# One hybrid mLSTM and windowed-attention layer: the load of the spread row factors queued behind the store of an attention block

## The chip, the cores and the metric

The kernel runs on one core of one Trainium2 chip, in one launch. The metric is device time in microseconds (us); lower is better. Several executions were timed, and one more was recorded by the hardware profiler.

## What is computed

The reference is one layer of a bidirectional encoder on a sequence of 4096 tokens of width 1024, in float32:

```python
hn = rms_norm(x, norm_w)
proj = hn @ w_in                     # 3856 columns
# group A: 4 heads x 128, short conv + SiLU on q and k, gated matrix memory
#          (chunks of 128), one scan in each direction, summed
# group B: 8 query heads / 2 key-value heads x 64, keys with |i - j| <= 128,
#          T5 bias, a sink logit per head
y = concatenate([y_a, y_b])          # each gated by silu of its own columns
out = rms_norm(x + y @ w_out, final_norm_w)
```

The change lies in the first pass, which makes group B's attention.

## The kernel before, in words

Float32 products are made of three (or two) float32r products of high and low parts, so TensorE has most of the work. There are three passes. `pass1` normalizes x, splits it into a high and a low part, makes q, k, v and the gate columns of group B, runs the attention, and writes two things to DRAM: the split, transposed x (`xT_d`) for the later passes, and the attention results (`at_d`), one [128, 512] block for each of 32 query blocks. Later passes make group A and the output.

**The steady loop of pass 1** (lines 608 to 620) runs over b = 0 to 12. x is handled in blocks of 256 tokens (16 of them), queries in blocks of 128 (two per x block), and attention in slots: one slot is one query block and one key-value head. In iteration b:

- `spread(b + 3)` (line 245) loads the 256 row factors of x block b+3 (the reciprocal root mean squares) from the DRAM buffer `rs_d` into all 128 partitions of the tile `rsb`. In iteration 0 it stands ahead of the loop (line 607).
- `load_rows(b + 4)` (line 222) loads rows of x (`xr`), and `norm_rows(b + 4)` (line 232) takes their squares on ScalarE, the factor on DVE and GpSimd, and writes it to `rs_d` with two small DMAs from GpSimd (line 243). Transposing the factors over partitions is what this trip through DRAM is for.
- A1: slots 4b and 4b+1, between the matmuls of `qproj(b + 1)` (line 523). `scale_raw(b + 3)` (line 251), on GpSimd, multiplies the raw, already transposed x (`xraw`) by `rsb`.
- A2: slots 4b+2 and 4b+3, between `kproj(b + 2)` and `vproj(b + 2)`. `splits(b + 3)` (line 257) splits the scaled `xraw` into `xT` (ScalarE line 263, GpSimd line 264), stores it to `xT_d` from GpSimd (line 277), and after its second and its fourth part loads a half of the next block's raw x (`load_raw(b + 4, h)`, line 229, SyncE, 512 KB each).

**The attention of a slot** is scores (line 358), softmax (361 to 375), transposes (386), and the product with v into one PSUM bank, `op` (line 400; the tag has one buffer). A slot's product is made in the slot behind it. ScalarE copies one half of `op` into the tile `ab` (line 412), and DVE adds the other half (line 413), which empties the bank. `ab` has one buffer. After the second head of a query block SyncE stores `ab` to `at_d` (line 415). The copy for the next query block must wait until that store has landed.

**The rings.** `x4` has 14 buffers, which `xT`, `xraw` and the transposed probabilities `pt` share; `rsb` has two buffers.

**What sets the order.** TensorE runs in the order of the code. On the other engines, SyncE's queue of loads and stores among them, a planner chooses the order; each engine then runs its list in order, and an instruction that waits holds all behind it on its queue. `behind(c, ins)` ties the instructions traced in its block to come after `ins` in their engine's list; it adds no wait on the hardware, and with `None` it does nothing. So SyncE's list between two stores is what the planner made of `spread`, `load_raw`, `load_rows` and the stores.

Of the kernel before, what the change touches and what calls it, by code (L numbers as in the profile page):

```python
# [122 lines left out]
def behind(c, ins):  # L123
    return c.tc.issue_after(ins.ins) if ins is not None else ExitStack()
# [43 lines left out]
def pass1(c):  # L168
    nc, tc, A = c.nc, c.tc, c.A
    NB = 16  # L170
    with ExitStack() as es:
# [42 lines left out]
        RAW, RSB, LAST = {}, {}, {}  # L214
# [30 lines left out]
        def spread(b):  # L245
            if b >= NB:
                return
            RSB[b] = wk.tile([128, 256], F32, tag="rsb", bufs=2, name=f"rsb{b}")
            nc.sync.dma_start(RSB[b], c.rs_d[b].partition_broadcast(128))

        def scale_raw(b):
            with behind(c, LAST["pool"]):
# [138 lines left out]
        def att_o(sl, i):  # L391
            n, kv = sl // 2, sl % 2
            js = ST[sl][1]
            if i >= len(js):
                return
            if i == 0:
                OP[sl] = c.ps("c", [128, 512], f"op{sl}")
            op, pt, vt = OP[sl], PT.pop((sl, i)), V[n - 1 + js[i]][:, kv, :]
            for z in range(2):
                nc.tensor.matmul(op, vt, pt[:, z, :], start=(i == 0 and z == 0),  # L400
                                 stop=(i == len(js) - 1 and z == 1))
            if i < len(js) - 1:
                return
            if kv == 0:
                AB[n] = wk.tile([128, 4, 128], F32, tag="ab", bufs=1, name=f"ab{n}")
            ab = AB[n]
            a = slice(0, 64) if kv == 0 else slice(64, 128)
            o = slice(64, 128) if kv == 0 else slice(0, 64)
            ov = op.rearrange("p (h g q) -> p h g q", h=2, g=4)
            av = ab.rearrange("p g (h q) -> p h g q", h=2)  # L410
            with tc.high_priority(offset=EV):
                nc.scalar.copy(av[a], ov[o])
                nc.vector.tensor_add(av[a], ov[a], av[a])  # L413
            if kv:
                nc.sync.dma_start(c.at_d[n], ab.rearrange("p g q -> p (g q)"))

        def slot(sl):
            T = lambda i: (lambda: att_t(sl, i))
            O = lambda i: (lambda: att_o(sl - 1, i))
            Sc = lambda g: (lambda: att_a(sl + 2, g))  # L420
            p = [Sc(0), O(0), Sc(1), T(0), O(1), Sc(2), T(1), O(2), Sc(3), T(2)]
            if sl == 0:
                p = [Sc(0), Sc(1), T(0), Sc(2), T(1), Sc(3), T(2)]
            if sl + 2 >= 2 * NCH:
                p = [O(0), T(0), O(1), T(1), O(2), T(2)]
            return p
# [175 lines left out]
        with behind(c, LAST["gather"]):  # L602
            load_rows(3)
            for h in range(2):
                load_raw(3, h)
        norm_rows(3, LAST["cast"])
        spread(3)
        for b in range(NB - 3):
            if b:
                spread(b + 3)  # L610
            load_rows(b + 4)
            s1 = slot(4 * b + 1)
            A1 = slot(4 * b) + [lambda: norm_rows(b + 4, LAST["act"])]
            A1 += s1[:5] + [lambda: scale_raw(b + 3)] + s1[5:]
            A2 = slot(4 * b + 2) + slot(4 * b + 3)
            interleave(qproj(b + 1), A1)
            f2, tu = kproj(b + 2) + vproj(b + 2), splits(b + 3)
            for p, u in zip((12, 20, 28, 36)[::-1], tu[::-1]):
                f2.insert(p, u)
            interleave(f2, A2)  # L620
        c.x7 = XT
        pieces = []
        for sl in range(4 * (NB - 3), 4 * NB):
            pieces += slot(sl)
        pieces += [(lambda i=i: att_o(2 * NCH - 1, i)) for i in range(3)]
        hooks = [(40, lambda: w2_load(0, 0)), (80, lambda: gate1(c, wk)), (100, lambda: gate2(c, wk)),
                 (104, lambda: w2_load(1, 512)), (113, lambda: gate3(c, wk)), (113, lambda: w2_load(2, 1024))]
# [898 lines left out]
```

## Time and profile before

| | us |
|---|---|
| median of 3 runs (2235.1 to 2237.13) | 2236.47 |
| the profiled execution's own time | 2239.41 |
| its span | 2237.7 |
| TensorE busy | 2168.3 (97%) |
| DVE, ScalarE, GpSimd busy | 1408.1, 1075.6, 609.5 |

The span is that of one profiled execution, from its first instruction to its last. An engine is busy while it computes; waiting and issuing DMAs is not counted. The granted clock is the share of full speed at which TensorE may run. SyncE (SP, or SPq for its queue) only issues DMAs here. A DMA has three moments: its issue, the time when its data moves, and its landing, of which a semaphore tells.

### The profile page before, as it was taken

To read this page: it belongs to the slowest core of one execution; us is meant where nothing else is said; L and a number is where in the kernel's file an instruction comes from. 1 tells how busy PE (TensorE), PEld (TensorE's weight loads), DVE (VectorE), ACT (ScalarE), POOL (GpSimd) and SP (SyncE) were. 2 spreads that over 40 slices of the span, in tenths; PEclk is the share of its full clock that TensorE was granted. 3 is DMA by queue.
4 is the path that set the end of the run, shared out by engine and by line. 5 is a ranking of instruction groups with operands and counts; after the bars stand their busy time and mean duration, and the time that the engine had idled before them with its cause. 6 is when DMAs were issued, how large, how long until landed. Compare 5 with 4: busy or idle time off the path is not lost.

```text
span 2237.7 us, 35209 instructions
## 1 busy us (share of the span) xinstructions
PE 2168.3 (97%) x12226; PEld 1879.7 (84%) x12226; DVE 1408.1 (63%) x3090; ACT 1075.6 (48%) x2711; POOL 609.5 (27%) x1059
## 2 busy tenths in 40 slices
PE   7999999999999999999999999999999999999997
PEld 6899999998788888888887888888888888888886
DVE  5677777777864665566567555555554443867776
ACT  5787787777743343334345343434443321333323
POOL 2555555553212211221122111111111111112222
PEclk9999999999999999999999999999999999999999
DMA  7542434422314442444166967876785899667774
GB/s 246 170 169 93 170 105 163 146 89 81 100 60 146 156 131 68 158 155 136 64 216 180 315 211 233 246 232 209 237 245 187 283 357 297 184 182 191 191 190 139
DMA packets 249126, 398.98 MB, mean 178 GB/s; under 512 B 21971, under 2 KB 128467, under 8 KB 248948
## 3 DMA queue, kind: packets, MB, share of 16 engines
q1 hardware_dynamic: 220628, 303.57, 43.5%
q0 software_dynamic: 28176, 92.96, 12.8%
q8 instruction: 96, 1.57, 0.3%
q14 instruction: 82, 0.67, 0.1%
q10 hardware_dynamic: 144, 0.20, 0.0%
HBM read 275.99 MB, written 120.67 MB: 177 GB/s over the span
## 4 chain that ended last, share of the span: by engine, by line
PE 71%; DMA 12%; DVE 5%; issue 5%; ACT 3%; POOL 2%; SPq 0%; POOLq 0%; DVEq 0%; ACTq 0%
PE up L855 15%; PE zp L1147 7%; PE op L1147 7%; PE qp L523 7%; PE v2p L828 7%; DMA xr<-x 5%; DMA at_d<-ab 3%; PE op L400 3%; PE zbp L158 3%; PE zbp L160 3%; PE zbp L159 3%; PE num L1100 2%; PE num L1099 2%; PE tp L386 2%; PE sp L358 2%
## 5 line engine op out<-in xcount | busy, mean ns | idle before, releaser
L855 PE MATMUL up<-xb,w 128*128 128x512 f32 x1344 | 338.5, 396 | 0.0
L1313 PE MATMUL o<-wo,yo 128*128 128x512 f32 (+1 forms) x1356 | 312.3, 392 | 0.0
L1313 PEld LDWEIGHTS o<-wo,yo 128*128 128x128 f32 x1356 | 253.2, 188 | 59.2
L855 PEld LDWEIGHTS up<-xb,w 128*128 128x128 f32 x1344 | 243.7, 188 | 47.2
L873 DVE SCALAR_TENSOR_TENSOR qk<-U,cw,qk 128x512 f32<-128x512 f32 x256 | 190.1, 754 | 92.5 <-ACT qk L871 88.6
L523 PE MATMUL qp<-xT,wqb 128*128 128x256 f32 x1536 | 246.5, 291 | 0.0
L523 PEld LDWEIGHTS qp<-xT,wqb 128*128 128x128 f32 x1536 | 218.3, 193 | 9.0 <-issue 0.9
L1147 PE MATMUL op<-w,xs 128*128 128x512 f32 x720 | 202.7, 409 | 2.9 <-ACT hs L1114 2.9
L1147 PE MATMUL zp<-w,xs 128*128 128x512 f32 x720 | 188.2, 402 | 2.3 <-DVE z L1156 2.3
L828 PE MATMUL v2p<-w,xb 128*128 128x512 f32 x672 | 158.1, 395 | 1.8 <-DMA xb<-xT_d 1.8
L1147 PEld LDWEIGHTS zp<-w,xs 128*128 128x128 f32 x720 | 131.0, 189 | 29.3 <-DVE z L1156 2.8
L828 PEld LDWEIGHTS v2p<-w,xb 128*128 128x128 f32 x672 | 125.9, 188 | 32.7 <-DMA xb<-xT_d 3.4
L1114 ACT ACTIVATE hs<-num,r 128x128 f32<-128x128 f32 x128 | 46.9, 367 | 213.8 <-DVE r L1111 185.2
L361 DVE CUSTOM_DVE_ANT_0 s<-sp,G 128x320 f32<-128x320 f32 (+1 forms) x256 | 122.7, 480 | 42.5 <-PE sp L358 39.3
L400 PE MATMUL op<-pt,v 128*128 128x512 f32 x376 | 122.2, 406 | 26.3 <-DVE ab L413 26.3
L1147 PEld LDWEIGHTS op<-w,xs 128*128 128x128 f32 x720 | 126.9, 190 | 24.3 <-ACT E L1068 3.3
L389 DVE TENSOR_TENSOR pt<-tp,pt 128x512 fp32r<-128x512 f32 x188 | 129.2, 688 | 26.1 <-ACT pt L388 24.7
L370 ACT ACTIVATE s<-s,st 128x320 f32<-128x320 f32 (+1 forms) x256 | 139.7, 549 | 10.1 <-DVE st L368 9.4
L388 ACT CAST pt<-tp 128x512 fp32r<-128x512 f32 x188 | 109.8, 586 | 59.0 <-PE tp L386 57.0
L358 PE MATMUL sp<-kk,q 128*128 128x320 f32 (+2 forms) x512 | 118.9, 314 | 0.0
L386 PE MATMUL tp<-ident,s 128*128 128x128 f32 x752 | 113.8, 274 | 1.5 <-DVE pt L389 1.2
L158 PE MATMUL zbp<-xc,w 128*128 128x512 f32 x256 | 101.5, 397 | 0.0
(273 smaller groups left out, 4444.0 us busy)
## 6 DMA issues: line engine op xcount, KB each, us to landing
xc<-xT_d SPq DMA_DIRECT2D x64, 512.0 KB, 7.9
xs<-xT_d SPq DMA_DIRECT2D x120, 256.0 KB, 6.3
xT_d<-xT POOLq DMA_DIRECT2D x104, 256.0 KB, 6.4
xb<-xT_d SPq DMA_DIRECT2D x48, 514.0 KB, 10.0
E<-m_d SPq DMA_DIRECT2D x64, 256.0 KB, 4.8
W<-w_d SPq DMA_DIRECT2D x64, 256.0 KB, 5.7
y<-y_d SPq DMA_DIRECT2D x32, 512.0 KB, 3.4
out<-xr POOLq DMA_DIRECT2D x31, 512.0 KB, 3.9
```

What stands on the lines that cost most here:

```text
L158: nc.tensor.matmul(out, wl, xh, start=first, stop=False)
L358: nc.tensor.matmul(sp[:, lo:hi], qt, kk[:, kv, z, col - 128 + lo:col - 128 + hi], start=(z == 0), stop=(z == 1))
L370: nc.scalar.activation(ps[g][:, kept(g)], ps[g][:, kept(g)], AF.Exp, bias=ng[:, g:g + 1], accum_out=rs[:, g:g + 1])
L386: nc.tensor.transpose(tp[:, g * 128:(g + 1) * 128], ps[g][:, j * 128:(j + 1) * 128], c.ident)
L389: nc.vector.tensor_sub(pt[:, 1, :], tp, f32(pt[:, 0, :]))
L400: nc.tensor.matmul(op, vt, pt[:, z, :], start=(i == 0 and z == 0), stop=(i == len(js) - 1 and z == 1))
L523: nc.tensor.matmul(qp, wq[k // 2][:, k % 2, w, m * 128:m * 128 + 128], x[k], start=(k == 0 and j == 0), stop=(k == KT - 1 and j == 2))
L828: nc.tensor.matmul(vp, a, wv[k // 2][:, k % 2, m, :], start=(k == 0 and j == 0), stop=(k == KT - 1 and j == 2))
L855: nc.tensor.matmul(up[:, 0:hi - lo], w[k // 2][:, k % 2, a, cs], x, start=(k == 0 and j == 0), stop=(k == KT - 1 and j == 2))
L873: nc.vector.scalar_tensor_tensor(acc, U[:, t:t + 512], cw[:, cm, t:t + 1], acc, ALU.mult, ALU.add)
L1147: nc.tensor.matmul(P[nm], XS[n](a, k), w[:, m, :], start=(k == 0 and j == 0), stop=(k == KT - 1 and j == 2))
L1313: nc.tensor.matmul(p, a[:, z, k, :], w[k // 2][:, k % 2, m, lo:hi], start=k == 0 and z == 1, stop=k == 3 and z == 0 and m == 0)
```

## The change

The load in `spread` is tied behind the store of attention results that was traced last; `LAST["at"]` keeps that store. Where none has been traced (`LAST.get("at")` is `None`, for the first spread) nothing is tied.

```diff
             RSB[b] = wk.tile([128, 256], F32, tag="rsb", bufs=2, name=f"rsb{b}")
-            nc.sync.dma_start(RSB[b], c.rs_d[b].partition_broadcast(128))
+            with behind(c, LAST.get("at")):
+                nc.sync.dma_start(RSB[b], c.rs_d[b].partition_broadcast(128))
...
             if kv:
-                nc.sync.dma_start(c.at_d[n], ab.rearrange("p g q -> p (g q)"))
+                LAST["at"] = nc.sync.dma_start(c.at_d[n], ab.rearrange("p g q -> p (g q)"))
```

## Rows read from the trace of the kernel before

**Rows 1.** The page, busy time of the engines.
```profile
PE 2168.3 (97%) x12226; PEld 1879.7 (84%) x12226; DVE 1408.1 (63%) x3090; ACT 1075.6 (48%) x2711; POOL 609.5 (27%) x1059
```
**Rows 2.** Windows: stretch, its length, each engine's busy time, PE clock, DMA share, GB/s.
```profile
95.00:515.00 420.00, 405.37 (x3055) 390.53 (x3054) 310.29 (x876) 329.91 (x906) 239.78 (x402) 1.00 0.38 132
```
**Rows 3.** Waits from 95 to 500 us: who, for whom, us, times, longest.
```profile
ACT ab L412 <- DMA at_d<-ab: 19.1, 10, 2.6
...
PE op L400 <- DVE ab L413: 14.6, 10, 2.1
```
**Rows 4.** Chain of waits up to 236 us: start, length, what.
```profile
225.19 8.76 DMA at_d<-ab
...
234.02 0.59 ACT ab L412
```
**Rows 5.** Landings: line 415 (95 to 500 us), its store at 136.4, line 249.
```profile
DMA to landing us min/median/max: 2.0/6.9/8.4
...
DMA to landing us min/median/max: 3.8/3.8/3.8
...
DMA to landing us min/median/max: 4.4/5.1/6.1
```
**Rows 6.** Timeline of SyncE's queue, 206 to 246 us: start, length, what it issues.
```profile
207.10 0.33 SPq L415 DMA_DIRECT2D at_d<-ab  x1
222.80 0.33 SPq L249 DMA_DIRECT2D rsb<-rs_d  x1
223.30 0.33 SPq L229 DMA_DIRECT2D xraw<-xt  x1
225.19 0.32 SPq L415 DMA_DIRECT2D at_d<-ab  x1
228.27 0.33 SPq L229 DMA_DIRECT2D xraw<-xt  x1
...
244.69 0.33 SPq L415 DMA_DIRECT2D at_d<-ab  x1
```
**Rows 7.** SyncE's own waits from 95 to 500 us.
```profile
SPq L249 <- DMA rs_d<-rstd: 164.5, 11, 15.9
```
**Rows 8.** Windows of 1 us each behind the spread's issue at 222.80.
```profile
226.00:227.00 1.00, 1.00 (x11) 1.00 (x10) 0.97 (x4) 0.95 (x4) 0.98 (x4) 1.00 0.92 92
...
228.00:229.00 1.00, 1.00 (x9) 0.97 (x8) 0.97 (x3) 1.00 (x5) 1.00 (x2) 1.00 1.07 428
```
**Rows 9.** Timelines of TensorE (last q projection of a block) and of ScalarE.
```profile
217.20 0.85 PE L523 MATMUL qp<-xT,wqb 128*128 128x256 f32 x5
...
230.75 0.64 ACT L263 CAST xT<-xraw 128x512 fp32r<-128x512 f32 x1
```
**Rows 10.** Timeline of ScalarE at another block; in brackets idle time before, and its releaser.
```profile
374.81 0.58 ACT L412 COPY ab<-op 64x512 f32<-64x512 f32 x1 [0.48 <-DMA at_d<-ab]
```
**Rows 11.** Windows: the q projection stretch of three blocks.
```profile
232.60:255.60 23.00, 20.88 (x150) 20.15 (x149) 13.81 (x41) 15.36 (x42) 9.83 (x17) 0.93 0.29 114
304.60:325.30 20.70, 19.42 (x150) 18.69 (x149) 13.82 (x41) 15.29 (x42) 10.14 (x17) 1.00 0.32 123
375.50:394.80 19.30, 19.30 (x149) 18.61 (x148) 13.76 (x41) 14.54 (x40) 9.87 (x17) 1.00 0.38 136
```
**Rows 12.** Timeline of GpSimd, 223 to 251 us.
```profile
223.45 1.47 POOL L277 DMA_DIRECT2D xT_d<-xT  x2
...
245.62 4.79 POOL L254 TENSOR_TENSOR xraw<-xraw,rsb 128x1024 f32<-128x1024 f32 x2
```
**Rows 13.** Timelines of SyncE, GpSimd and TensorE at the start of the loop.
```profile
74.54 4.63 SPq L249 DMA_DIRECT2D rsb<-rs_d  x2
...
79.20 4.68 POOL L254 TENSOR_TENSOR xraw<-xraw,rsb 128x1024 f32<-128x1024 f32 x2 [7.10 <-DMA rsb<-rs_d]
...
83.62 0.73 PE L400 MATMUL op<-pt,v 128*128 128x512 f32 x2 [2.24 <-DVE ab L413]
```

## The prediction

> **What bounds the kernel now.** I read the page first: TensorE is busy for 97% of the span [rows 1], so a change shows in the time only where it moves TensorE's idle time or its clock. The edited line runs only in the first pass, so I then cut the span into stretches. From 95 to 515 us, which holds the steady blocks of that pass, TensorE is busy for 405.37 of 420 us [rows 2]: 14.6 us are lost. The table of waits puts a name on them: 10 waits of the attention-value product (line 400) for the addition that empties its PSUM bank (line 413) make 14.6 us. One step behind it, ScalarE's copy into the result tile `ab` (line 412) waited 10 times, 19.1 us in all, for the landing of the store of that same tile [rows 3]. So the stall is no lack of compute: `ab` has one buffer, its store to DRAM lands late, and the copy of the next query block may not overwrite it sooner.
>
> The chain of waits shows one of these, the worst. The store of an even block, issued at 225.19, took 8.76 us to land, and the copy started right behind that at 234.02 [rows 4]. Over the 23 stores of the stretch the landing goes from 2.0 to 8.4 us with a median of 6.9 [rows 5] (the profile has no landing for a few, that one among them; the chain supplies it). Landing by landing the long ones are all stores of even blocks; the odd ones take 2.0 to 3.8 us [rows 5].
>
> Why only the even ones? SyncE's own timeline of one period [rows 6] has this order: odd store, spread, first half of the raw x, even store, second half. The even store goes out at 225.19, right after its data is ready, so SyncE does not hold it. What is wrong is what went out just ahead, the spread at 222.80 and 512 KB of raw x at 223.30. SyncE's waits say why these two come so late: the spread waited for the row factors to land in DRAM, 164.5 us over 11 blocks, 15.9 us at worst [rows 7]. Everything queued behind it is held as well. When it is released, it and the raw x are bunched in front of the store.
>
> The spread is dear for its bytes. Between 226 and 227 us the DMA engines are 92% busy and move only 92 GB/s, whereas from 228 on, with everything else in flight, they move 428 GB/s at 107% [rows 8] (about 100% is full). From the length of the poor stretch ahead of 228 I put the spread at 1.5 to 2 us of all engines, an estimate. The raw x adds 512 KB at 428 GB/s, 1.2 us.
>
> **The change part by part.** It is one edge: the spread may not be queued before the latest result store that was traced. I count which one that is. The spread for x block b+3 is traced at the top of iteration b; the last store traced by then is that of query block 2b-2, in the first half of the iteration before. That is the even store that today follows the spread by 2.4 us [rows 6]. So 11 steady spreads move behind the very store that they delay, one more (the second of the start) moves behind the store of block 0, and the first is not bound to anything. No instruction is added or removed.
>
> *The even store.* With the spread no longer ahead, the first half of the raw x is no longer held by it. Its buffer is from the ring of 14 that also holds the split x tiles. I take it as free when the q projection has read the oldest of these, at about 218.05 [rows 9]; the trace has no such wait, so the bounds are 218 and today's 223.3. At the early end it has landed before the store is issued, at the late end it still stands ahead, but without the spread. Then the store should land like the odd ones, 2.0 to 3.8 us after 225.19, at about 229; at the late end some 1.8 us earlier than today, at 232. ScalarE could use it at 231.39, when its cast before the copy ends [rows 9]. Even the late end leaves 0.7 us of the 2.63 us that this copy waits, and TensorE's longest wait is 0.5 us shorter than the copy's [rows 3]. There is a block in the trace that shows this: at 374.81 the copy waited only 0.48 us [rows 10], and TensorE was busy throughout what followed [rows 11]. So all ten stalls go: **-14.6 us**. Bounds: -7 (the stores land half as much earlier) to -14.6.
>
> *What is late next.* The block with the short wait answers it: its q projection stretch takes 19.30 us with TensorE busy throughout, where the usual one takes 20.70 with 19.42 busy [rows 11]. No other engine appears behind the stall. DVE (13.76) and ScalarE (14.54) have room there.
>
> *The clock.* Behind the worst stall the granted clock falls to 0.93 over the stretch from 232.6 us, and the same 150 matmuls take 20.88 us of busy time and not 19.42 [rows 11]. Without that stall it should not fall: **-1.5 us**; bounds 0 and -1.5.
>
> *The moved spread.* It goes out at about 225.6 and takes 4.4 to 6.1 us to land [rows 5]: 231.7 at most. GpSimd needs it at 245.62, when it starts the scaling [rows 12]. The cover is 14 us; without it the whole delay of 2.8 us would go onto GpSimd's queue, once a block. Behind it on SyncE stand the second half of the raw x and the next rows of x, which keep their places. They lose at most the 2 us of its transfer; the second half, issued at 228.27, is needed after the first has been scaled. Cost nil.
>
> *The start.* The first two spreads stand together at 74.54. Here GpSimd waited 7.10 us for the first and TensorE 2.24 us for the `ab` addition that came late because of it [rows 13]. Today nothing follows this first spread for 4 us; with the second one moved, raw x follows at once. With traffic behind it a spread lands in 5.1 us by the median, and this one took the 4.4: **+0.7 us**, bounds 0 and +1.7 (6.1 less 4.4).
>
> Sum: -14.6 - 1.5 + 0.7 = **-15.4 us**. The profiled execution took 2239.41 us (span 2237.7), so 2224.0 by its own count. The median of the runs is 2236.47, 2.9 us less; the same difference gives **2221.1 us**. A measurement of this kernel can tell about 0.2% (4.5 us) from no change.
>
> **The rivals.** *Half of it.* The room left by the spread is taken by GpSimd's stores of the split x, two of which start at 223.45 and share the same 16 engines [rows 12]; from 228 on the engines are full [rows 8]. The store lands at some 231 to 233 and half the stall stays: -7.3, or 2229. Against it: at 228 the store would already have been flowing. *No change.* The edge could fall on a store already ahead of the spread, leaving the order as it is; or the store is late because of all the traffic around it, whichever comes first: 2236.5. For that: the full engines from 228 on. Against: the odd stores, and the 1.5 us or more in which the engines carry almost nothing but the spread. The Trainium skill (DMA: Bandwidth & Descriptors, Issuing engines are not separate DMA queues) states such a rule: transfers from all issuing engines share the same DMA engines and interleave, so that starting them differently saves only issue time. The even stores in the trace speak against reading it so far, since one queue's own order shows in their landing.
>
> *Slower.* The spread is pushed so far back that GpSimd waits for it: if it ended behind the odd store (244.69 in this period), it would land at about 250 and the scaling at 245.62 would start 4.5 us late, 12 times: up to +54 us, 2290, if all reached TensorE. The point from which this decides is an issue after about 240.5. Against it: the count above, which gives the even store.
>
> **How the numbers follow.** All stalls gone: 0.73. Half: 0.13. No change: 0.08. Slower: 0.06, with smaller losses from a different order of other engines' work. Faster by over 0.2% is 0.73 + 0.13 = 0.86. The range runs from 2216 (the full -16.1 without the loss at the start, and 4 us for a shifted order of work) to 2232 (a little less than the half case). What it leaves out is the last two cases, 0.14, and some 0.05 of the first two.
>
> **What would show it.** The even stores land in 2 to 4 us; SyncE issues the first raw half several us before them and the spread right behind; the waits of line 412 for the store and of line 400 for line 413 are gone from 95 to 500 us; the clock stays at 1.00; GpSimd still does not wait for the spread. Wrong it would be if the even stores still took 7 us, if the spread stood elsewhere, or if new TensorE waits appeared in these blocks.

## The result and the profile after

The median of four runs is **2215.14 us** (2212.8 to 2218.53) against 2235.78 us (four runs, 2235.1 to 2237.13): ratio 0.9908 [0.9891, 0.9925], 20.6 us less. A second measurement of the same kernel, below, gave 19.2 us less. The predicted 2221.1 had the direction and most of the size; the median lies 0.9 us below the range. The lines of the kernel after are one higher than those of before from line 250 on.

The page of the kernel after, against [rows 1]: TensorE has the same work in a shorter span (2216.8 us).

```profile
PE 2165.7 (98%) x12226; PEld 1880.3 (85%) x12226; DVE 1407.0 (63%) x3090; ACT 1075.4 (49%) x2711; POOL 607.3 (27%) x1059
```

The timeline of SyncE's queue over one period of the kernel after, against [rows 6] (the period that is shown there):

```profile
215.67 0.33 SPq L229 DMA_DIRECT2D xraw<-xt  x1
222.72 0.33 SPq L416 DMA_DIRECT2D at_d<-ab  x1
223.21 2.12 SPq L250 DMA_DIRECT2D rsb<-rs_d  x1
225.80 0.33 SPq L229 DMA_DIRECT2D xraw<-xt  x1
228.71 0.89 SPq L222 DMA_DIRECT2D xr<-x  x2
238.29 0.33 SPq L416 DMA_DIRECT2D at_d<-ab  x1
```

The order is the predicted one: the first half of the raw x goes out 7 us ahead of the even store, the spread stands right behind that store, and the second half, then x's next rows, follow. The first half has not landed when the store goes out: it took 10.0 us from its issue at 215.67. TensorE, DVE, ScalarE and GpSimd run the same lists of instructions as before, so whatever changed came from SyncE's order.

The waits of the kernel after from 95 to 484 us, against [rows 3] (first line), and the landings of its 23 stores of attention results in that stretch, against [rows 5]:

```profile
ACT ab L413 <- DMA at_d<-ab: 0.3, 1, 0.3
...
DMA to landing us min/median/max: 2.0/4.2/6.4
```

Of ten waits of the copy, 19.1 us, one of 0.3 us is left, and TensorE's waits for the addition (14.6 us) are gone from this stretch. On the whole page 13.2 us of them are left, 4.0 at the start (below) and 9.2 in the last blocks of the pass, which the spread does not reach:

```profile
L401 PE MATMUL op<-pt,v 128*128 128x512 f32 x376 | 121.5, 404 | 13.2 <-DVE ab L414 13.2
```

The landings fell from a median of 6.9 us to 4.2. The even stores by themselves went from 6.9 to 8.8 us (the chain's 8.76 among them) to 4.2 to 6.4, as far as the profile has their landings, not to the 2 to 4 us that I expected of them, but it was enough.

The stretch of the q projection behind what was the worst stall, against the first line of [rows 11]:

```profile
230.14:249.44 19.30, 19.30 (x151) 18.78 (x150) 13.57 (x42) 14.36 (x40) 9.86 (x17) 1.00 0.34 130
```

23.00 us have become 19.30, with the granted clock at 1.00 and TensorE never idle.

**How much is the loop's?** Since TensorE's list is the same, one instruction can be found in both traces. Three matmuls serve as marks, one ahead of the first spread, one early in the loop, one at the end of the steady blocks. TensorE's timelines, first before, then after:

```profile
62.72 1.48 PE L523 MATMUL qp<-xT,wqb 128*128 128x256 f32 x11
...
92.62 0.62 PE L523 MATMUL qp<-xT,wqb 128*128 128x256 f32 x4
...
515.45 0.51 PE L523 MATMUL qp<-xT,wqb 128*128 128x256 f32 x3
```

```profile
63.71 1.48 PE L524 MATMUL qp<-xT,wqb 128*128 128x256 f32 x11
...
95.32 0.63 PE L524 MATMUL qp<-xT,wqb 128*128 128x256 f32 x4
...
499.25 0.51 PE L524 MATMUL qp<-xT,wqb 128*128 128x256 f32 x3
```

At the first mark the kernel after is 0.99 us late, by chance, since nothing moved has run yet. At the second it is 2.70 us late: in this pair of traces the start costs 1.7. From the second to the third it takes 403.93 us and not 422.83: the steady loop gives **-18.9 us**. I use this span between the second and the third mark for every kernel that keeps TensorE's list.

### The profile page after: what moved, and what is told of

It is laid out like the page before. It is cut to its first block, busy times and chain, and to the rows that moved or that the text cites. A ratio compares the mean times of both kernels' runs of the same rounds, so it can differ in the third digit from the quotient of the medians.

```text
span 2216.8 us, 35208 instructions
## 1 busy us (share of the span) xinstructions
PE 2165.7 (98%) x12226; PEld 1880.3 (85%) x12226; DVE 1407.0 (63%) x3090; ACT 1075.4 (49%) x2711; POOL 607.3 (27%) x1059
## 4 chain that ended last, share of the span: by engine, by line
PE 77%; DMA 9%; issue 5%; DVE 4%; ACT 3%; POOL 2%; SPq 1%; POOLq 0%; DVEq 0%; ACTq 0%
PE up L856 15%; PE op L1148 7%; PE zp L1148 7%; PE qp L524 7%; PE v2p L829 7%; DMA xr<-x 5%; PE op L401 4%; PE tp L387 3%; PE sp L359 3%; PE zbp L158 3%; PE zbp L160 3%; PE zbp L159 3%; PE num L1101 2%; PE num L1100 2%; PE o L1314 2%
## 5 line engine op out<-in xcount | busy, mean ns | idle before, releaser
L401 PE MATMUL op<-pt,v 128*128 128x512 f32 x376 | 121.5, 404 | 13.2 <-DVE ab L414 13.2
```

## The experiments

Two theories stood against each other at first. *Order*: the store lands late because of what SyncE issued just ahead of it. *Traffic*: it lands late because the DMA engines are full then, whatever the queue. And one question on the gain: is it the waits alone?

**The first raw half alone goes ahead.** The spread is tied behind the load of the first raw half, and still stands ahead of the even store:

```diff
             ld = nc.sync.dma_start(t, A["xt"][b, :, 4 * h:4 * h + 4, :])
+            if h == 0:
+                LAST["raw"] = ld
...
+            with behind(c, LAST["raw"] if b > 4 else None):
                 nc.sync.dma_start(RSB[b], c.rs_d[b].partition_broadcast(128))
```

> The kernel before, with the spread tied behind the first half of the raw x instead of behind the store: odd store, raw x, spread, even store. Queue-order theory (the even store lands late because of what stands ahead of it on SyncE's queue, and its ten stalls are the gain): only the spread is ahead now, 1.5 to 2 us of the engines, so the even stores land 4 to 5.5 us after issue, the copy of line 412 waits 0.5 us or less, and the time is 2217 to 2223. Rival, the spread alone does the harm: landings stay above 6 us, at least half of the ten TensorE waits stay, 2226 or more. Rival, all the traffic of these microseconds does it in whatever order: as the kernel before, 2236.

Measured: 2222.49 us (2221.12 to 2223.38) against 2236.88, ratio 0.993 [0.9913, 0.9946]. The waits from 95 to 500 us and SyncE's order (lines here are three higher than before):

```profile
ACT ab L415 <- DMA at_d<-ab: 2.5, 2, 1.7
...
PE op L403 <- DVE ab L416: 1.5, 2, 1.2
```

```profile
216.63 0.33 SPq L229 DMA_DIRECT2D xraw<-xt  x1
222.34 0.33 SPq L252 DMA_DIRECT2D rsb<-rs_d  x1
223.68 2.10 SPq L418 DMA_DIRECT2D at_d<-ab  x1
```

From mark to mark the loop gained 16.3 of the 18.9 us. Two waits stay, because the even stores, with the spread issued right ahead of them and the raw half not yet landed (9.1 us from 216.63), still take up to 7.8 us. So in this order most of the gain comes from not holding the raw x back behind the spread, and the last 2.6 us from the spread's own place.

**The store first, the raw half behind it.** The kernel after, with the first raw half tied behind the even store as well:

```diff
+            with behind(c, LAST.get("at") if h == 0 and b > 4 else None):
                 nc.sync.dma_start(t, A["xt"][b, :, 4 * h:4 * h + 4, :])
```

> The changed kernel with the first half of the raw x also tied behind the even store: even store, raw x, spread. The raw x is read no earlier than in the kernel before. Queue-order theory: nothing stands ahead of the store, it lands in 2 to 4 us, all ten TensorE waits are gone, the time is that of the change within 4 us, 2211 to 2219. Rival, the gain comes from reading the raw x earlier, out of the crowded stretch: landings of 6 us and more come back and half the stalls with them, 2225 or more.

Measured: 2237.34 us (2234.22 to 2242.61), ratio 1.0007 [0.9993, 1.002]: no gain. The landings were the best of all (first line, the stores from 95 to 500 us), but a new wait stood in place of the old (second line, its waits):

```profile
DMA to landing us min/median/max: 2.0/3.4/4.4
...
PE tp L388 <- DVE pt L391: 9.6, 11, 0.9
```

Here the planner also gave ScalarE, DVE and GpSimd other orders, and a wait of the transposes for the probability tile came with them, most of a microsecond in each block. No copy waits for a landing any more, but TensorE's waits for the addition are not all gone as expected: 3.5 us of 14.6 are left. The time is the one that the rival gave, the landing the one that the theory gave. The landing shows that the store lands early when it is ahead of the bunch; the time says nothing on the change, as it holds two causes.

**Two buffers for `ab`, nothing moved.** The kernel before; the room comes from `rsb` and three small tables that go into a larger tile:

```diff
-            RSB[b] = wk.tile([128, 256], F32, tag="rsb", bufs=2, name=f"rsb{b}")
+            RSB[b] = wk.tile([128, 256], F32, tag="rsb", bufs=1, name=f"rsb{b}")
...
-                AB[n] = wk.tile([128, 4, 128], F32, tag="ab", bufs=1, name=f"ab{n}")
+                AB[n] = wk.tile([128, 4, 128], F32, tag="ab", bufs=2, name=f"ab{n}")
```

> The kernel before with two buffers for the result tile ab (room for it: one buffer for the spread factors, and gate bias and sink tiles moved into the spare end of another buffer). The store may land as late as it likes. Theory, the gain is the ten waits for the landing and nothing else: even stores still land in 7 to 9 us, no copy waits for them, the ten TensorE waits are gone; by the recorded idle time 14.6 us and 1.5 of clock, by the shift of TensorE's own instructions about 17 and 1.7: 2216 to 2221. Rival, a good part of the gain comes from the DMA order itself: 2226 or more.

Measured: 2217.65 us (2213.97 to 2222.66), ratio 0.991 [0.989, 0.993]. Its landings from 95 to 500 us, and the marks of its loop:

```profile
DMA to landing us min/median/max: 2.0/6.1/9.1
```

```profile
94.20 0.64 PE L523 MATMUL qp<-xT,wqb 128*128 128x256 f32 x4
...
498.18 0.52 PE L523 MATMUL qp<-xT,wqb 128*128 128x256 f32 x3
```

The stores land late as before, nothing waits for them, and the loop takes 403.98 us: -18.85, the change's gain to 0.1 us, by another way. So the gain is that of the waits alone, and not of calmer DMA engines as such.

**The even stores issued by ScalarE.** The kernel before, the spread and the raw x unmoved:

```diff
-                nc.sync.dma_start(c.at_d[n], ab.rearrange("p g q -> p (g q)"))
+                q = nc.scalar if n % 2 == 0 and 2 <= n <= 22 else nc.sync
+                q.dma_start(c.at_d[n], ab.rearrange("p g q -> p (g q)"))
```

> The kernel before with the eleven even stores that follow a spread issued from ScalarE's queue. Spread and raw x go out as before, just ahead in time, but on another queue. Queue-order theory: the store need not wait behind them, lands in 3 to 5 us, the stalls are gone; ScalarE pays some 0.3 us of issue and a wait of 0.8 us for the DVE addition, 11 times, mostly beside other work: 2217 to 2227. Rival, the rule that all issuing engines share the DMA engines and interleave: landings stay at 6.5 us and more, stalls stay, 2234 or more.

Measured: 2236.07 us (2229.36 to 2239.7), ratio 0.999 [0.9979, 1.0002]. From 95 to 500 us the waits, then in one period ScalarE's timeline and windows of 1 us:

```profile
ACT ab L412 <- DMA at_d<-ab: 16.8, 8, 3.0
...
PE op L400 <- DVE ab L413: 13.2, 7, 2.5
```

```profile
229.01 0.33 ACTq L416 DMA_DIRECT2D at_d<-ab  x1
...
236.87 0.58 ACT L412 COPY ab<-op 64x512 f32<-64x512 f32 x1 [1.65 <-DMA at_d<-ab]
```

```profile
228.00:229.00 1.00, 1.00 (x11) 1.00 (x9) 0.94 (x3) 0.50 (x2) 0.98 (x3) 1.00 1.48 14
229.00:230.00 1.00, 1.00 (x9) 0.91 (x8) 0.96 (x2) 0.99 (x4) 1.00 (x2) 1.00 0.19 12
230.00:231.00 1.00, 1.00 (x11) 1.00 (x10) 1.00 (x4) 0.96 (x3) 0.98 (x3) 1.00 0.63 59
...
232.00:233.00 1.00, 1.00 (x11) 1.00 (x10) 0.97 (x3) 1.00 (x5) 1.00 (x2) 1.00 1.06 432
```

Issued by another engine the store is as late as ever: its landings go from 5.3 to 9.1 us. What SyncE had issued at 227.25 and 227.74, the spread and the raw x, has not landed at 229.01. The engines move 12 to 59 GB/s until 231, at shares of time from 0.19 to 1.48 that say little of the bytes, and are full soon after, at 432 GB/s. So the order of SyncE's queue by itself is not what holds the store up. What is left is the traffic in the engines, whoever issued it. The Trainium skill (DMA: Bandwidth & Descriptors, Issuing engines are not separate DMA queues) states that DMAs issued by different engines run on the same DMA engines and interleave. This run agrees with it.

**The change measured again.**

> The changed kernel once more, for the size of the step. Its first profile gains 18.9 us in the steady loop and loses 1.7 at the start; the rest of its 20.6 us (median) came from places outside the pass where the profile of the kernel before was unlucky. If that is so the median is 2216 to 2221, 16 to 20 us below the kernel before of the same chip. Rival: the change has a further effect in the later passes, 2212 to 2215 again, and again no wait of line 828 for xb and no clock fall near 1200 us.

Measured: 2216.62 us (2215.55 to 2218.62) against 2235.86, ratio 0.9921 [0.9908, 0.9934]. The marks of its loop are at 95.02 and 499.44, that is 404.42 us or -18.4. The time is inside the expected 2216 to 2221, and inside the predicted range: two measurements of one kernel differ by 1.5 us, more than the 0.9 by which the first one missed it.

**The first moved spread stays.** The change, but the second spread of the start keeps its old place next to the first:

```diff
-            with behind(c, LAST.get("at")):
+            with behind(c, LAST.get("at") if b > 4 else None):
```

> The change without its first moved spread: the spread of x block 4 keeps its place directly behind that of block 3, so no raw x is read behind the first spread. Theory: the first spread lands in 4.4 us again and not in 6.4, GpSimd waits 7.1 us for it and not 8.9, TensorE's first wait falls from 3.96 to 2.2 us and the clock does not fall there: 1.7 us better than the change at 95 us of the span, perhaps 1.7 more by the clock, 2211 to 2218. Rival: the longer first wait has another cause, and nothing changes.

Measured: 2218.43 us (2215.06 to 2219.83), ratio 0.9923 [0.9908, 0.9938]. The waits at the start, in the timelines of GpSimd and TensorE, first of the kernel after, then of this one; [rows 13] has those of before:

```profile
81.95 4.64 POOL L255 TENSOR_TENSOR xraw<-xraw,rsb 128x1024 f32<-128x1024 f32 x2 [8.86 <-DMA rsb<-rs_d]
...
86.33 0.73 PE L401 MATMUL op<-pt,v 128*128 128x512 f32 x2 [3.96 <-DVE ab L414]
```

```profile
81.21 4.69 POOL L255 TENSOR_TENSOR xraw<-xraw,rsb 128x1024 f32<-128x1024 f32 x2 [7.06 <-DMA rsb<-rs_d]
...
85.63 0.73 PE L401 MATMUL op<-pt,v 128*128 128x512 f32 x2 [2.22 <-DVE ab L414]
```

With the two spreads together again, both waits are back at their old 7.1 and 2.2 us. That fits the predicted cause, but the size is not the 1.7 us of one pair. In the five traces where no raw x goes out right behind the first spread (before, this run, two buffers alone, the raw half ahead, the store by ScalarE) that spread took 4.4 to 5.5 us to land and TensorE waited 2.17 to 3.07 us; in the five where it does, 5.5 to 6.5 and 2.89 to 3.96. The means of TensorE's wait are 2.4 and 3.4: some 1.0 us, with single runs that overlap. That cannot be seen in the time of a run, and this version (2218.43) is not shown to be faster than the change (2216.62 beside it).

**Both: the change and two buffers for `ab`.**

> The change and two buffers of ab together. Both remove the same ten waits, so the gains do not add: in the steady loop within 1 us of either alone, by the time 2214 to 2221. Rival: the change has an effect of its own beside the store's landing, then some 3 us or more better than two buffers alone.

Measured: 2221.26 us (2217.01 to 2221.68), ratio 0.9935 [0.9921, 0.9949]. Its loop has the marks at 94.28 and 498.24, 403.96 us: -18.9. The gains do not add, as both remove the same ten waits. The median is 4.6 us above that of the change measured beside it and just over the expected 2221; the loop shows nothing of that, and I leave it open.

**The spread behind the odd store.** The slower rival: the spread is traced after the first slots of its iteration, so that it is tied to the odd store and comes just ahead of its use.

```diff
-            if b:
-                spread(b + 3)
...
-            A1 = slot(4 * b) + [lambda: norm_rows(b + 4, LAST["act"])]
+            A1 = slot(4 * b) + ([lambda: spread(b + 3)] if b else []) + [lambda: norm_rows(b + 4, LAST["act"])]
```

> The change with the spread traced one store later, behind the odd store, just ahead of its use: the slower rival of the prediction made real. GpSimd waits for the spread about 4 to 6 us in each of 12 blocks. If that reaches TensorE it is up to 54 us, 2270; if the slack of GpSimd behind the scaling takes it (the splits follow some 8 us later) the time stays within 6 us of the change, 2211 to 2223. The spread then stands ahead of the raw x and some 17 us ahead of the even store, so the store should land in 4 to 7 us.

Measured: 2252.12 us (2245.48 to 2262.45), ratio 1.0083 [1.0053, 1.0113], slower. The waits from 95 to 500 us, and one period of SyncE's queue:

```profile
ACT ab L413 <- DMA at_d<-ab: 34.6, 8, 8.2
...
POOL xraw L255 <- DMA rsb<-rs_d: 33.7, 10, 3.6
...
PE op L401 <- DVE ab L414: 30.9, 7, 7.7
```

```profile
278.23 1.05 SPq L250 DMA_DIRECT2D rsb<-rs_d  x1
288.81 0.33 SPq L229 DMA_DIRECT2D xraw<-xt  x1
295.98 0.32 SPq L416 DMA_DIRECT2D at_d<-ab  x1
```

GpSimd now does wait for the spread, 3.4 us a block, but TensorE does not wait for GpSimd: its waits, 30.9 us, are again those for `ab`. The even store takes up to 14.2 us, with no spread anywhere near it (the one shown landed in 3.9 us). The entry added to A1 also shifted TensorE's own matmuls of the q projection among the slots, and DVE and ScalarE got other orders, so this run does not price the move alone.

## Why the prediction was right, and where it was not

*The bound, the cause, the count.* All three held: TensorE's ten stalls, behind the copy into `ab`, behind the even store; the spread goes behind that store, and the raw half is freed (at 215.67, the q projection's end, by the early bound). The two-buffer run shows that these waits are all of the loop's gain. One step to the landing was wrong: at this early end I had the raw half landed before the store is issued, from 1.2 us of transfer, and it took 10.0 us. So the even stores still met it and landed in 4.2 to 6.4 us and not like the odd ones. The waits went all the same, but for one of 0.3 us: ScalarE comes back to `ab` about then and not sooner.

*The stalls, -14.6.* This is the step that failed, by its size: the ten stalls cost 17.2 us. I took the recorded idle time of the matmuls as all that a stall can cost, and gave it a lower bound and no upper one. Followed from stall to stall in both traces, each matmul behind a stall moved by 0.2 to 0.3 us more than its idle time. One of them in TensorE's timelines, first before, then after:

```profile
480.43 0.64 PE L523 MATMUL qp<-xT,wqb 128*128 128x256 f32 x4
482.20 0.73 PE L400 MATMUL op<-pt,v 128*128 128x512 f32 x2 [1.13 <-DVE ab L413]
482.77 0.64 PE L523 MATMUL qp<-xT,wqb 128*128 128x256 f32 x4
```

```profile
465.61 0.65 PE L524 MATMUL qp<-xT,wqb 128*128 128x256 f32 x4
466.09 0.65 PE L401 MATMUL op<-pt,v 128*128 128x512 f32 x2
466.58 0.63 PE L524 MATMUL qp<-xT,wqb 128*128 128x256 f32 x4
```

The same work takes 2.34 us and then 0.97, 1.37 less, with 1.13 of idle time. The rest is in the records of busy time: the pair behind the stall takes 0.73 and not 0.65, and without the stall it starts 0.17 us before the recorded end of the matmuls ahead of it. The trace of before has a row that comes closer and that I passed over, the waits of TensorE's weight loads (PEld) for the same product from 95 to 500 us:

```profile
PEld op L400 <- DVE ab L413: 16.9, 11, 2.3
```

The eleventh is at the very block that I took as free of a stall, the one with the copy's wait of 0.48 us. TensorE's record is busy throughout there, and yet the stretch from 375.56 to 376.74 takes 0.24 us less in the kernel after. 16.9 is the better price. It would have given a sum of -17.7 and 2218.8 us, and with the same allowances a range reaching down to 2214, with the result inside, though 3.4 us of that result belong to the rest below.

*The clock, -1.5.* Held: inside the stretch that was at 0.93, the matmuls from 235.94 to 240.23 took 4.29 us, and they take 2.75 in the kernel after, 1.5 less. 17.2, 0.24 and 1.5 make the loop's -18.9, to 0.1 us.

*The start, +0.7.* The first pair of traces has the bound, +1.7: the spread, with raw x right behind it, landed like the slowest of the steady ones, and not like the median, and GpSimd's wait for it grew from 7.10 to 8.86 us. The repeat gave 1.2 by the same marks. Over all traces it is about 1.0, so the cause and the size held as far as the runs can tell.

*The rest.* Loop and start make -17.2; the medians differ by 20.6 and 19.2. The 2.0 to 3.4 us between lie outside the steps of the prediction. Behind the third mark, where TensorE has the same list in all of these kernels, the profiled executions took 1722.2 us before and 1717.6 after, but also 1718.1 in the run with ScalarE's queue (2234.9 less 516.80), which is no faster than before, and 1715.1 in the repeat. So this stretch differs as much where the spread and its order are untouched, and none of the rest is shown to be the change's. Of the 5.2 us by which the first measurement beat the sum of -15.4, the stalls account for 2.6 and the eleventh block for 0.2, the start takes 1.0 back, and the rest is 3.4.

*"No change" and the rule.* I set the rule on shared engines, which the prediction has from the Trainium skill, aside because the even stores alone landed late. The run with ScalarE's queue speaks for it: with the same traffic around it the store is late whoever issues it. The change helps nevertheless, since it alters what is in the engines when the store arrives, not only who issues it. My description of the traffic was right, my use of it against the rule was not.

*The slower rival.* The same line traced a few statements later gives 0.8% slower, with the other orders that came with it, so what the position alone does stays open. GpSimd's wait, the rival's mechanism, came near its price (3.4 us a block against 4.5), but no wait of TensorE is put down to it. It may still have a part: it puts off GpSimd's small stores of the row factors, which stand behind the scaling, and so brings them close to the raw half (last section). That is not shown.

## What to carry to other kernels

If the copy into a single-buffered tile waits for that tile's own store, look at what was issued in the microseconds ahead of that store on any queue; either let the store go first, or give the tile a second buffer, and expect one gain, not two. Price a stall of TensorE by the idle time of its weight loads and not by that of its matmuls, which was 16.9 us here against 14.6 for a cost of 17.2, and give a removed stall an upper bound too. Before moving a store to another queue, read from the windows what else is in the engines then: moving it gave nothing here.

## What was unexpected of the hardware

The poor microseconds, in which the DMA engines are busy and move little, are not the spread's alone. In the kernel after, windows of 1 us show them at a time when no spread is in flight, and fuller ones once it has gone out at 223.21:

```profile
219.00:220.00 1.00, 1.00 (x10) 1.00 (x10) 0.79 (x3) 0.87 (x2) 0.07 (x2) 1.00 0.82 25
...
221.00:222.00 1.00, 1.00 (x12) 1.00 (x10) 0.92 (x4) 0.79 (x2) 1.00 (x3) 1.00 0.77 33
...
224.00:225.00 1.00, 1.00 (x11) 1.00 (x11) 1.00 (x4) 0.96 (x4) 0.98 (x3) 1.00 0.80 303
```

At 219 us the engines are 82% busy with 25 GB/s. In flight are the first raw half, issued at 215.67, and the two small stores of the row factors, issued by GpSimd at 212.06 and landed 8.6 to 9.0 us after their issue. The same spread that I priced at 1.5 to 2 us of all engines now runs among 303 GB/s. In the run with the spread behind the odd store the raw half was issued 0.7 us after such a pair of factor stores, and that is the period in which the even store took 14.2 us. This points to the factor stores as what makes their neighbours slow, but no run took them away, so it is a reading and not shown.
